# Head 1's keys and queries by seven products in a hybrid decoder trunk; where the replaced block of x is made, and when the out-projection's weight sums run

## The chip, the cores and the metric

The kernel runs on one core of one Trainium2 chip. The metric is the device time of one execution in microseconds (us). A core has five instruction queues that matter here: TensorE (PE, matmuls; PEld is its weight load), VectorE (DVE), ScalarE (ACT), GpSimd (POOL) and SyncE (SP, which only issues DMAs). Each queue runs its instructions in the order in which they stand, and an instruction that waits holds everything behind it in its queue. DMAs are issued from SP, ACT and POOL.

## The reference

One layer: RMS norm, one input projection, three token mixers on disjoint head groups, gates, one output projection with a residual, and a final RMS norm. 512 tokens and 16 learned meta tokens make 528 columns.

```python
h = rms_norm(x, norm_w)
proj = h @ w_in
(dq, dk, dv, dz, db, da, gq, gk, gv, gz, gl, fq, fk, fv, fz, ff) = split_cols(proj)
o_dn  = gated_head_norm(gated_delta_rule_chunked(...), dz, dn_norm_w)   # 6 heads x 128
o_gla = gated_head_norm(gla_chunked(...), gz, gla_norm_w)               # 5 heads, dk 64, dv 128
o_fox = forgetting_attention(fq * 128**-0.5, fk, fv, log_f) * silu(fz)  # 5 heads x 128
x = x + concat([o_dn, o_gla, o_fox]) @ w_out
return rms_norm(x, final_norm_w)[:, N_META:]
```

## The kernel before

**Precision and the unit of work.** Every large product is made from operands split into two parts, hi and lo, and three matmuls: hi by hi, hi by lo, lo by hi. A block is 128 columns of `w_in`; it is loaded in two halves of 512 KB (`load_half`, line 144): SP loads `raw`, ACT casts it into `whi` (line 165), DVE subtracts and gives `wlo` (line 166). `raw`, `whi` and `wlo` have two buffers each. Rows of such halves run through the whole program, and PE eats them in order. x itself stands split in SBUF, as `xh[k]` and `xl[k]` for 16 rows k of 128 channels.

**Order of the program.** First `dz` of four heads and the gates; then DeltaNet in two groups of three heads (`dn_keys`, `dn_values`, `dn_queries`, `dn_inverse`, `dn_mix`); then the five gates `gz` of GLA (line 1304 on); then GLA in three pairs of heads (`gla_pair`); then five heads of forgetting attention (`fox_head`); then the output projection. A scheduler puts the instructions of each queue into their order from the program and a timeline of its own; a few rules pin places: `PLACE` says behind which matmul of which block a matmul of GLA stands, `behind` and `later` do the same by distance, `high_priority` lets splits go first.

**The inverse.** `dn_inverse` inverts 32-row triangles by 60 short DVE operations on the tile `ab` (lines 740 and 742), each of which needs the one before it. The result goes to DRAM and comes back in another layout: `sc<-ab` (744), then `iv<-sc` and `xm<-sc` (747, 749), all issued on ACT's queue, so that ACT stands still between 744 and 747 until the copy has landed. For the second group of heads this runs while PE makes the gates `gz`. In the profile block 25 is `gz` of GLA head 1, 28 that of head 4, 29 the first keys of GLA (`gk`), and `whi29_1` the second half of block 29.

**A gate.** `gate_z` (402): DVE takes the projection out of PSUM (`zgz`, 403), POOL takes a maximum (`stgz`, 385), ACT makes three activations (386 to 388), DVE one product (389).

**Seven products.** `inproj_pair` (558) makes two blocks together from seven half-size products instead of eight, after Winograd's scheme: the columns of x are cut into two halves of 264, its rows k into 0 to 7 and 8 to 15, the weights into four halves. It needs sums of weights in DRAM (`ti`), made early by DMAs on POOL, copies and then adding DMAs (`in_jobs`, `steps_of`, 490 and 492); sums of x (`t`, made by `x_sums` in `gla_pair`); and for its fifth product a replaced block: `x_last` (543) overwrites the upper half of `xh[k]`, `xl[k]`, k below 8, by differences of x. From then on x can't be used whole. `load_half` lets the weight-sum DMAs go in portions: each half allows `rate` cost units of the list `chores`, 1 for a copy and 1.6 for a sum, tied by `paced` behind that half's split in the queue's order.

Before the change the pairs begin with `fv` and `fz` of head 1 (`SKIP` = 1); head 0's four blocks and head 1's keys `fk` and queries `fq` are made whole, with 96 matmuls of 264 columns and 48 of 512. `x_last` stands behind head 1's queries: eight loads `xe` on POOL, then per block two operations on ACT and two on DVE. The output projection uses seven products for eight of its 16 rows, with weight sums `tw`.

## Time and profile before

| | |
|---|---|
| median of three executions | 999.3 us (999.12 to 1000.33) |
| the profiled execution | 997.56 us, span of its core 995.9 us |
| mean granted clock of PE | 0.997 |
| busy PE, DVE, ACT, POOL | 980.4, 666.8, 475.3, 249.0 us |
| gates `gz` of GLA | within 340 to 400 us |
| head 1's keys and queries | 612.08 to 639.4 us |
| pairs by seven products | 639.4 to 815 us |

Times in a row are us from the start of the span; a mean in ns stands in the third view of a group. "Idle before" is the time that the engine did nothing before that row, with an arrow to what ended it. A share of DMA is the mean of the 16 DMA engines. PE's matmuls are pipelined, so rows overlap, and the distance between starts is what one costs.

### The profile page before, as it was taken

The numbers are of one execution on the slowest core, as the hardware profiler recorded it, in microseconds if no ns is written. First come the engines' busy times: TensorE is split into PE (matmuls) and PEld (weight loads), VectorE is DVE, ScalarE is ACT, GpSimd is POOL, SyncE is SP. The second block draws the span as 40 slices with busy tenths as digits, with TensorE's granted clock in tenths as the row PEclk, the third lists the DMA queues.
The fourth block names the chain that finished last, engine by engine and source line by source line (L and its number), as shares of the span: only waits on it lengthen the run. The fifth ranks groups of instructions, "written<-read, shape, count | busy, mean of one in ns | idle before, by whom it ended". The sixth has DMA issues, their size and how long they took to land.

```text
span 995.9 us, 19769 instructions
## 1 busy us (share of the span) xinstructions
PE 980.4 (98%) x7774; PEld 896.6 (90%) x7774; DVE 666.8 (67%) x1443; ACT 475.3 (48%) x1043; POOL 249.0 (25%) x293
## 2 busy tenths in 40 slices
PE   9999999999999999999999999999999999999996
PEld 7899999899999888899999988799999998888885
DVE  6356786966567895434675847776766676877573
ACT  7653533334456234334546444555555554454353
POOL 0031423322233244301313223221221134000060
PEclk9999999999999999999999999999999999999998
DMA  9754666777547688844847866565454577355634
GB/s 346 263 193 168 210 216 238 172 181 173 116 113 169 140 215 198 298 130 144 209 143 190 186 178 178 176 200 161 168 172 135 182 267 273 106 190 199 202 106 169
DMA packets 67489, 186.05 MB, mean 187 GB/s; under 512 B 13725, under 2 KB 16973, under 8 KB 66692
## 3 DMA queue, kind: packets, MB, share of 16 engines
q1 hardware_dynamic: 41920, 121.86, 36.0%
q0 software_dynamic: 16576, 56.83, 23.9%
q10 hardware_dynamic: 8900, 6.10, 2.2%
q8 instruction: 61, 1.00, 0.4%
q14 instruction: 32, 0.26, 0.1%
HBM read 174.07 MB, written 56.69 MB: 232 GB/s over the span
## 4 chain that ended last, share of the span: by engine, by line
PE 70%; DVE 7%; DMA 5%; ACT 3%; issue 2%; POOL 1%; ACTq 0%; DVEq 0%; POOLq 0%
PE pp L240 28%; PE pp_a L571 8%; PE pa L1392 5%; PE pq L1392 4%; PE pt L1392 4%; PE ps L1392 2%; PE pp_b L571 2%; PE pp_d L571 2%; PE pp_c L571 2%; DVE wlo L166 2%; DMA sc<-ab 1%; DMA zd<-gqk 1%; PE pr L1392 1%; PE pss L1041 1%; ACT whi L165 1%
## 5 line engine op out<-in xcount | busy, mean ns | idle before, releaser
L240 PE MATMUL pp<-xh,wlo 128*128 128x264 f32 (+2 forms) x1120 | 272.9, 306 | 2.2 <-DVE wlo L166 2.2
L240 PE MATMUL pp<-xh,whi 128*128 128x264 f32 (+2 forms) x1120 | 273.9, 306 | 0.0
L240 PE MATMUL pp<-xl,whi 128*128 128x264 f32 (+2 forms) x1120 | 272.9, 306 | 0.0
L165 ACT CAST whi<-raw 128x1024 fp32r<-128x1024 f32 x131 | 137.1, 1047 | 157.0 <-PE pp L240 81.2
L166 DVE TENSOR_TENSOR wlo<-raw,whi 128x1024 fp32r<-128x1024 f32 x131 | 160.6, 1226 | 72.8 <-ACT whi L165 64.2
L240 PEld LDWEIGHTS pp<-xh,wlo 128*128 128x128 f32 x1120 | 182.6, 189 | 12.1 <-DVE wlo L166 3.6
L240 PEld LDWEIGHTS pp<-xh,whi 128*128 128x128 f32 x1120 | 182.6, 189 | 9.4 <-ACT whi L165 0.4
L240 PEld LDWEIGHTS pp<-xl,whi 128*128 128x128 f32 x1120 | 182.7, 189 | 8.9 <-issue 0.4
L385 POOL TENSOR_SCALAR stc<-cv 128x528 f32<-128x528 f32 (+1 forms) x18 | 28.9, 1607 | 144.9 <-DVE cv L613 124.4
L613 DVE SCALAR_TENSOR_TENSOR cv<-pb,cpk,cv 128x528 f32<-128x528 f32 (+1 forms) x54 | 41.1, 761 | 0.8
L1417 POOL TENSOR_TENSOR acc<-acc,fw 128x512 f32<-128x512 f32 x4 | 5.8, 1483 | 117.4 <-ACT sqf L1414 117.4
L571 PE MATMUL pp_a<-t,whi 128*128 128x264 f32 (+1 forms) x224 | 30.5, 284 | 0.0
L1392 PE MATMUL pa<-wloo,oh 128*128 128x512 f32 x72 | 28.7, 398 | 0.0
L571 PE MATMUL pp_a<-xh,whi 128*128 128x264 f32 x112 | 28.4, 288 | 0.0
L571 PEld LDWEIGHTS pp_a<-t,whi 128*128 128x128 f32 x224 | 27.9, 189 | 0.5
L1392 PE MATMUL pa<-whio,ol 128*128 128x512 f32 x72 | 28.4, 394 | 0.0
L571 PE MATMUL pp_a<-xl,whi 128*128 128x264 f32 x112 | 28.3, 287 | 0.0
L385 POOL TENSOR_SCALAR stdz<-zdz 128x512 f32<-128x512 f32 x6 | 11.3, 1885 | 62.1 <-DVE zdz L403 62.0
L165 ACT CAST whis<-raws 128x1024 fp32r<-128x1024 f32 x16 | 16.3, 1048 | 21.2 <-PE pq L1392 10.8
L166 DVE TENSOR_TENSOR wlos<-raws,whis 128x1024 fp32r<-128x1024 f32 x16 | 19.2, 1223 | 10.7 <-ACT whis L165 10.6
L1392 PE MATMUL pa<-whio,oh 128*128 128x512 f32 x72 | 26.0, 400 | 0.0
L740 DVE TENSOR_TENSOR ab<-ab 51x30 f32<-51x30 f32 (+14 forms) x60 | 21.2, 354 | 6.4 <-DMA ab<-scr 4.2
(509 smaller groups left out, 2138.6 us busy)
## 6 DMA issues: line engine op xcount, KB each, us to landing
raw<-in_w_in SPq DMA_DIRECT2D x103, 512.0 KB, 3.7
ti<-in_w_in POOLq DMA_DIRECT2D x42, 512.0 KB, 5.5
raw<-ti SPq DMA_DIRECT2D x28, 512.0 KB, 3.3
tw<-in_w_dn POOLq DMA_DIRECT2D x24, 512.0 KB, 5.9
ti<-ti POOLq DMA_DIRECT2D x14, 512.0 KB, 6.3
rawo<-in_w_out SPq DMA_DIRECT2D x13, 512.0 KB, 3.2
raws<-tw SPq DMA_DIRECT2D x12, 512.0 KB, 3.9
xt<-in_xtok SPq DMA_DIRECT2D x8, 512.0 KB, 8.9
```

Source lines behind the costliest of these rows:

```text
L165: pace[0] = A.copy(hi, raw).ins
L166: pace[1] = V.tensor_tensor(out=lo, in0=raw, in1=hi.bitcast(F32), op=ALU.subtract).ins
L240: mm = PE.matmul(p_[:, :nt], wt[:, j * m : (j + 1) * m], xx[k][:, t0 : t0 + nt], start=(k == 0 and wt is hi and xx is xh), stop=(k == KT - ...
L385: maxes.append(G.tensor_scalar_max(t, src, LOW).ins)
L571: m = PE.matmul(p_[:, cols], wt[:, j * P : (j + 1) * P], xx[j][part_][:, cols], start=first and i == 0, stop=i == len(todo) - 1, skip_grou ...
L613: V.scalar_tensor_tensor(out=c, in0=pb[:, t0 + w : w + T], scalar=cwc[:, blk, w : w + 1], in1=c, op0=ALU.mult, op1=ALU.add)
L740: V.tensor_tensor(out=t3, in0=a3[:, j + 1 :, j : j + 1].to_broadcast([NN * 4 + H, m, j]), in1=a3[:, j : j + 1, 0:j].to_broadcast([NN * 4 + ...
L1041: mm = PE.matmul(ps[o0 : o0 + n, b * n : b * n + n], kx[rr, k0 : k0 + n], qx[rr, q0 : q0 + n], start=True, stop=True)
L1392: mm = PE.matmul(p_, o_[:, s], w_, start=(first and n == 0), stop=(last and n == 2), skip_group_check=True)
L1417: G.tensor_tensor(out=acc[tb, cc], in0=acc[tb, cc], in1=fw[cc], op=ALU.mult)
```

## The change

`SKIP` becomes 0, so head 1's `fk` and `fq` become the first pair, with four more halves of `ti`. As this pair comes before x could be replaced, its products have another order: the one on replaced x is the last of seven, and the one for the unused columns gets its own bank `e`. The differences of x are made in `x_early`, two blocks in each of the first three gates `gz` of GLA and one in each of the last two, and go to a DRAM tensor `x3`; `x_last` only fetches them, by 16 DMAs of 132 KB on POOL behind head 0's `fz`. `PLACE` pins the scores of GLA pair 2 within the new pair. The portions allowed to `chores` drop from 1.4 to 0.35 a half from head 1 on, and once the first pair is in the program a sum of weights waits for the split and doesn't only stand behind it.

```diff
-SKIP = 1
+SKIP = 0
...
+        "pss21": (('pair', 0), 22),
+        "pss22": (('pair', 0), 38),
+        "pss23": (('pair', 0), 54),
+        "pss24": (('pair', 0), 72),
+        "pss25": (('pair', 0), 90),
+        "pss26": (('pair', 0), 108),
+        "pg02": (('pair', 0), 128),
...
-        "pss23": (('fk', 1), 60),
-        "pss24": (('fk', 1), 80),
-        "pss25": (('fk', 1), 90),
-        "pgo2": (('pair', 0), 8),
...
-                paced(G.dma_start(out=out_, in_=in_, accum_op=ALU.add, max_dma_last_dim=2048))
+                x = G.dma_start(out=out_, in_=in_, accum_op=ALU.add, max_dma_last_dim=2048)
+                if ("pair", 0) in head:
+                    tc.add_manual_dep(x.ins, pace[1].name, mybir.DependencyInfo(
+                        mybir.DependencyClass.Sync, mybir.DependencyReason.DATA), reason="paced")
+                else:
+                    paced(x)
...
+    x3 = drp.tile([NK, P, T], F32, name="x3")
+
+    def x_early(k):
+
+        r, c = row(f"xe{k}")[:, :T], row(f"xc{k}", F32R)[:, :T]
+        nc.gpsimd.dma_start(out=r.rearrange("p (i t) -> p i t", i=2), in_=xT[:, k : k + 9 : 8, HT:])
+        x12, x22 = r[:, :HT], r[:, HT:]
+        A.activation(x12, x12, AF.Copy, scale=nwc[:, k : k + 1])
+        V.scalar_tensor_tensor(out=x22, in0=x22, scalar=nwc[:, k + 8 : k + 9], in1=x12, op0=ALU.mult,
+                               op1=ALU.subtract)
+        A.copy(c[:, :HT], x22)
+        V.tensor_tensor(out=c[:, HT:], in0=x22, in1=c[:, :HT].bitcast(F32), op=ALU.subtract)
+        nc.gpsimd.dma_start(out=x3[k], in_=c.bitcast(F32))
+
     def x_last():
 
         for k in range(NK):
-            r = row(f"xe{k}")[:, :T]
-            nc.gpsimd.dma_start(out=r.rearrange("p (i t) -> p i t", i=2), in_=xT[:, k : k + 9 : 8, HT:])
...
-            A.copy(xh[k][:, HT:], x22)
-            V.tensor_tensor(out=xl[k][:, HT:], in0=x22, in1=xh[k][:, HT:].bitcast(F32), op=ALU.subtract)
+            for x, o in ((xh, 0), (xl, HT)):
+                nc.gpsimd.dma_start(out=x[k][:, HT:].bitcast(F32), in_=x3[k][:, o : o + HT])
...
-        product(a, w_in[b2, 1], sums("t4"), cols=dead)
-        A.activation(c2[:, dead], a[:, dead], AF.Copy, scale=-1.0)
+        if n > 0:
+            product(a, w_in[b2, 1], sums("t4"), cols=dead)
+            A.activation(c2[:, dead], a[:, dead], AF.Copy, scale=-1.0)
+        else:
+            e = bank("e")
+            product(e, w_in[b2, 1], sums("t4"), True, cols=dead)
+            A.copy(c2[:, dead], e[:, dead])
+            replaced()
+            V.scalar_tensor_tensor(out=c2[:, dead], in0=a[:, dead], scalar=-1.0, in1=c2[:, dead],
+                                   op0=ALU.mult, op1=ALU.subtract)
...
+            done["fz", h] = inproj(("fz", h), meta=False)
+            x_last()
             gate_z("fz", h)
-            evac(inproj(("fk", H1)), ahead_[H1][:, 0])
-            evac(inproj(("fq", H1), meta=False), ahead_[H1][:, 2], scale=float(P) ** -0.5)
-            x_last()
...
-    AHEAD = {(0, -1): (1.4, (-1, -2, -3, -4, -5, -6, -7), (0, 1, 2, 3))}
+    AHEAD = {(0, -1): (1.4, (-1, -2, -3, -4, -5, -6, -7, -8), (0, 1, 2, 3)), ("f", 1): (0.35,)}
...
     for h in range(G1):
         gate_z("gz", h)
+        for i in ((0, 1), (2, 3), (4, 5), (6,), (7,))[h]:
+            x_early(i)
```

The order that the scheduler makes of it, at three places. DVE between the two splits of block 27, while PE makes gate 3 (names: `wlo` the low half of a weight, `ab` the inverse, `zgz1` gate 1, `xe` and `xc` the blocks of x as loaded and as split). Before:

```order
L166 TENSOR_TENSOR wlo27_0_4802<-raw27_0_4799,whi27_0_4801 128x1024
L742 TENSOR_TENSOR ab1_4071<-ab1_4071 51x15x16
L740 TENSOR_TENSOR ab1_4071<-ab1_4071 51x238
L742 TENSOR_TENSOR ab1_4071<-ab1_4071 51x14x17
L740 TENSOR_TENSOR ab1_4071<-ab1_4071 51x234
L742 TENSOR_TENSOR ab1_4071<-ab1_4071 51x13x18
L740 TENSOR_TENSOR ab1_4071<-ab1_4071 51x228
L742 TENSOR_TENSOR ab1_4071<-ab1_4071 51x12x19
L403 TENSOR_TENSOR zgz2_4789<-pp26_0_4726,rstd_102 128x512
L740 TENSOR_TENSOR ab1_4071<-ab1_4071 51x220
L166 TENSOR_TENSOR wlo27_1_4833<-raw27_1_4830,whi27_1_4832 128x1024
```

And now:

```order
L166 TENSOR_TENSOR wlo27_0_4853<-raw27_0_4850,whi27_0_4852 128x1024
L766 TENSOR_TENSOR ab1_4073<-ab1_4073 51x240
L768 TENSOR_TENSOR ab1_4073<-ab1_4073 51x15x16
L392 TENSOR_TENSOR zgz1_4736<-zgz1_4736,stgz1_4738 128x512
L766 TENSOR_TENSOR ab1_4073<-ab1_4073 51x238
L558 SCALAR_TENSOR_TENSOR xe2_4745<-xe2_4745,cpk_94 128x264
L768 TENSOR_TENSOR ab1_4073<-ab1_4073 51x14x17
L766 TENSOR_TENSOR ab1_4073<-ab1_4073 51x234
L561 TENSOR_TENSOR xc2_4746<-xe2_4745,xc2_4746 128x264
L768 TENSOR_TENSOR ab1_4073<-ab1_4073 51x13x18
L766 TENSOR_TENSOR ab1_4073<-ab1_4073 51x228
L166 TENSOR_TENSOR wlo27_1_4884<-raw27_1_4881,whi27_1_4883 128x1024
```

Between the splits stood eight operations of the inverse and the evacuation of gate 2; now there are seven, with gate 1's product and the two operations of block `xe2`.

ACT around the copy of the finished inverse (`whi28_0` to `whi29_1` are casts of successive halves, `stgz3` gate 3, `sc` the copy in DRAM). Before:

```order
L165 CAST whi28_0_4873<-raw28_0_4871 128x1024
L165 CAST whi28_1_4904<-raw28_1_4902 128x1024
L386 ACTIVATE stgz3_4863<-stgz3_4863 128x512
L744 DMA sc21_4143<-ab1_4071 51x1024
L387 ACTIVATE stgz3_4863<-stgz3_4863 128x512
L388 ACTIVATE stgz3_4863<-stgz3_4863 128x512
L165 CAST whi29_0_4951<-raw29_0_4949 128x1024
L747 DMA iv1_4145<-sc21_4143 128x12x32
L749 DMA xm1_4147<-sc21_4143 32x3x32
L165 CAST whi29_1_5006<-raw29_1_5004 128x1024
```

And now:

```order
L165 CAST whi28_1_4962<-raw28_1_4960 128x1024
L557 ACTIVATE xe4_4833<-xe4_4833,cpk_94 128x264
L560 CAST xc4_4834<-xe4_4833 128x264
L770 DMA sc21_4145<-ab1_4073 51x1024
L165 CAST whi29_0_5017<-raw29_0_5015 128x1024
L557 ACTIVATE xe5_4841<-xe5_4841,cpk_94 128x264
L773 DMA iv1_4147<-sc21_4145 128x12x32
L775 DMA xm1_4149<-sc21_4145 32x3x32
L560 CAST xc5_4842<-xe5_4841 128x264
L165 CAST whi29_1_5072<-raw29_1_5070 128x1024
```

The copy `sc` stands behind the same half, `whi28_1`; gate 3's activations, which stood around it, have gone further back, and parts of blocks 4 and 5 of x stand around it in their place, one of them (`xc5`) between the two read-backs and `whi29_1`.

POOL from gate 0's maximum on (`ti` are the input projection's weight sums). Before:

```order
L385 TENSOR_SCALAR stgz0_4648<-zgz0_4646 128x512
L490 DMA ti_680<-ti_680 256x512 x2
L385 TENSOR_SCALAR stgz1_4719<-zgz1_4717 128x512
L490 DMA ti_680<-ti_680 256x512 x2
L385 TENSOR_SCALAR stgz2_4791<-zgz2_4789 128x512
```

And now:

```order
L388 TENSOR_SCALAR stgz0_4650<-zgz0_4648 128x512
L555 DMA xe0_4657<-in_xT 128x2x264
L493 DMA ti_680<-ti_680 256x512
L555 DMA xe1_4665<-in_xT 128x2x264
L562 DMA x3_683<-xc0_4658 128x528
L493 DMA ti_680<-ti_680 256x512
L388 TENSOR_SCALAR stgz1_4738<-zgz1_4736 128x512
L555 DMA xe2_4745<-in_xT 128x2x264
```

The load of `xe2` stands behind gate 1's maximum, which itself now stands behind the store of block 0 to `x3`.

More of the change, by code (lines that the diff above doesn't have):

```diff
@@ L567, in product @@
             third[0] += 1
-            hi, lo = load_half(src, f"{b1}_{len(order)}", raws[0] if third[0] % 3 == 0 and 0 < n and h < FOX_HEADS - 1 else None)
+            hi, lo = load_half(src, f"{b1}_{len(order)}", raws[0] if third[0] % 3 == 0 and 1 < n and h < FOX_HEADS - 1 else None)
             todo = [(hi, j, i) for j in range(NK) for i in range(2)] + [(lo, j, 0) for j in range(NK)]
@@ L1018, in scores @@
             ref = gv[:, :, 0, s - 1 : s].to_broadcast([R, npair, s])
-            V.tensor_tensor(out=dv[:, :, 1, :], in0=gv[:, :, 1, :], in1=ref, op=ALU.subtract)
+            x = V.tensor_tensor(out=dv[:, :, 1, :], in0=gv[:, :, 1, :], in1=ref, op=ALU.subtract)
+            if p == 2 and li == 0:
+                kqs.append(x.ins)
             if s > 1:
```

19 lines of the change are left out of this document (8 added, 11 removed).

## The prediction

> **What bounds the kernel now.** First the page's busy times, then who keeps TensorE (PE) waiting.
>
> ```profile
> PE 980.4 (98%) x7774; PEld 896.6 (90%) x7774; DVE 666.8 (67%) x1443; ACT 475.3 (48%) x1043; POOL 249.0 (25%) x293
> ...
> PE pp L240 <- DVE wlo L166: 2.2, 4, 0.7
> ```
>
> PE is busy for 980.4 of 995.9 us, and its longest named wait, for the low half of a split weight (`wlo`, line 166), adds up to 2.2 us. So a change of the time has to be PE work that goes, or a new place where PE waits. Next, busy time by stage; the columns are PE, PEld, VectorE (DVE), ScalarE (ACT), GpSimd (POOL), clock, DMA share, GB/s.
>
> ```profile
> 340.00:400.00 60.00, 59.49 (x295) 49.65 (x294) 43.85 (x98) 23.75 (x33) 26.09 (x21) 1.00 0.80 190
> 612.00:640.00 28.00, 27.04 (x326) 23.16 (x328) 21.74 (x47) 14.05 (x29) 9.27 (x9) 1.00 0.60 162
> 640.00:815.00 175.00, 174.99 (x1423) 170.64 (x1410) 124.50 (x299) 96.61 (x200) 35.85 (x36) 1.00 0.55 180
> ```
>
> The three rows are the stages that the change touches: GLA's gates, where blocks of x will be made; head 1's keys and queries, where they are made now; and the pairs of blocks by seven products. PE has no idle time to give in the first or the third (59.49 of 60, 174.99 of 175). But the first is not free of limits: DVE is busy there for 43.85 us. Third, the chain of waits, which in this stretch leaves PE.
>
> ```profile
> 384.63 8.81 DMA sc<-ab
> ...
> 394.65 1.06 ACT whi L165
> 395.73 1.24 DVE wlo L166
> 397.01 6.84 PE pp L240 x49
> ```
>
> This is the place that decides my forecast. The DRAM copy of the finished 32-row inverses (`sc<-ab`) is issued by ACT at 384.63; ACT then waits in its own queue for that copy, because the next thing it has to issue reads it back; only then does it make `whi` of block 29's second half (394.65), DVE makes `wlo` (395.73), and PE starts that half at 397.01. PE stands at the end of a chain that begins with DVE's last `ab` operation.
>
> **The matmuls that go and come.** Durations are of this profiled execution.
>
> ```profile
> 111.73 5.82 PE pp L240 x48
> ...
> 702.68 2.94 PE pp_d L571 x24
> ...
> 870.94 11.12 PE pq L1392 x48
> ```
>
> Each row is a run of matmuls without a gap: 48 of 264 columns in 5.82 us, 24 of a product in 2.94, 48 of 512 columns in 11.12. Head 1's keys are 96 of the first kind, 11.64 us, its queries 48 of the last, 11.12: 22.76 us. Seven products are 7 x 2.94 = 20.58. The term is **-2.2 us**. Whether splits keep up with 2.94 us a product (seven now where there were four) is answered by the stage row 640:815: seven such pairs ran there with PE busy for 174.99 of 175. I take nothing for it; bounds 0 and +1 us, the latter being PE's idle time in row 612:640.
>
> **The stall that goes with the blocks of x.** Now they are made between 616 and 654, and once they hold up PE.
>
> ```profile
> 629.42 0.52 ACT L548 ACTIVATE xe<-xe,cpk 128x264 f32<-128x264 f32 x1 [4.93 <-DMA xe<-in_xT]
> 631.43 1.23 DVE L166 TENSOR_TENSOR wlo<-raw,whi 128x1024 fp32r<-128x1024 f32 x1 [4.06 <-ACT whi L165]
> 631.12 0.40 PE L240 MATMUL pp<-xh,wlo 128*128 128x512 f32 x1
> ...
> 632.71 0.50 PE L240 MATMUL pp<-xh,wlo 128*128 128x512 f32 x1 [0.53 <-DVE wlo L166]
> 633.04 0.40 PE L240 MATMUL pp<-xh,whi 128*128 128x512 f32 x1
> 633.66 0.46 PE L1041 MATMUL pss<-kq 64*32 64x32 f32 x32 [0.22 <-DVE kq L1027]
> 634.33 0.46 PE L1041 MATMUL pss<-kq,kq 64*32 64x32 f32 x32 [0.22 <-DVE kq L1027]
> 634.72 0.50 PE L240 MATMUL pp<-xl,whi 128*128 128x512 f32 x1
> ```
>
> ACT sits 4.93 us before an `xe` block whose load has not landed; the `whi` behind it in ACT's queue is late, DVE waits 4.06 us for that, and PE runs dry. From 631.12 to 634.72 PE issues five matmuls of 512 columns (5 x 11.12 / 48 = 1.16 us) and two groups of scores (633.66 to 634.72, less two waits of 0.22: 0.62), and took 3.60 us: 1.8 us are lost. After the change nothing of x is computed there, only fetched, so the term is **-1.8 us** (0 to -1.8; I take the whole, because ACT and DVE lose 8 x (0.52 + 0.41 + 0.48 + 0.42) = 14.6 us of work there and get three more splits, 3 x 2.3 = 6.9). The sixteen fetches into x wait for the last projection that reads x whole (`fz` of head 0), and the product that reads them is now the last of the seven, six products or 17.6 us later. On POOL's queue eight of them stand ahead of the `MEMSET` of GLA pair 2's score tile, which DVE needs here:
>
> ```profile
> 608.86 0.29 DVE L1008 COPY_PREDICATED a<-lmk,psd 128x128 f32<-128x128 uint8 x1
> ```
>
> `fz` is 48 matmuls of 512 columns, 11.1 us, and ends where row 612:640 begins, so its first row of x is used at 601 at the latest and each further one 0.7 us on: the eighth fetch can go at 604 and the memset follows, four before its use. Cost 0; if a fetch had to wait for the weight sums queued ahead on POOL, each microsecond past 608.9 would be one on PE, since DVE's splits queue behind it.
>
> **What GLA's gates have to take.** Eight blocks are now made there, two instructions each on ACT and DVE. The same work today:
>
> ```profile
> L548 ACT ACTIVATE xe<-xe,cpk x8: 501/515/517, 621.8 to 651.4; 128x264 f32<-128x264 f32 x8
> L549 DVE SCALAR_TENSOR_TENSOR xe<-xe,cpk x8: 479/484/1048, 637.9 to 652.7; 128x264 f32<-128x264 f32 x8
> ...
> L554 DVE TENSOR_TENSOR xl<-xe,xh x8: 419/424/434, 639.7 to 653.7; 128x264 fp32r<-128x264 f32 x8
> ...
> DMA to landing us min/median/max: 3.2/5.1/6.8
> ```
>
> A block costs DVE 0.484 + 0.424 = 0.91 us and ACT 0.93, and its load lands 5.1 us after issue (3.2 to 6.8). By the order of instructions five of the eight blocks stand on DVE ahead of the end of the `ab` chain, and one evacuation (0.67) moves behind it. DVE has little room there:
>
> ```profile
> 360.26 2.70 POOL L385 TENSOR_SCALAR stgz<-zgz 128x512 f32<-128x512 f32 x1 [5.76 <-DVE zgz L403]
> ...
> 364.09 0.40 DVE L740 TENSOR_TENSOR ab<-ab 51x240 f32<-51x240 f32 x1
> 365.06 0.69 DVE L389 TENSOR_TENSOR zgz<-zgz,stgz 128x512 f32<-128x512 f32 x1 [0.57 <-ACT stgz L388]
> ...
> 366.42 1.21 DVE L166 TENSOR_TENSOR wlo<-raw,whi 128x1024 fp32r<-128x1024 f32 x1
> ...
> 375.99 0.69 DVE L389 TENSOR_TENSOR zgz<-zgz,stgz 128x512 f32<-128x512 f32 x1 [0.76 <-ACT stgz L388]
> ...
> 383.79 0.18 DVE L742 TENSOR_TENSOR ab<-ab 51x30 f32<-51x30 f32 x1
> 384.62 0.63 ACT L386 ACTIVATE stgz<-stgz 128x512 f32<-128x512 f32 x1 [4.69 <-POOL stgz L385]
> 384.63 0.26 ACTq L744 DMA_DIRECT2D sc<-ab  x1
> ...
> 393.45 0.39 ACTq L747 DMA_DIRECT2D iv<-sc  x1
> ```
>
> Between 344 and 384 it stood still only before the two gate products, 0.57 and 0.76 us, and the chain ended at 383.97. Work alone moves that end by 5 x 0.91 - 0.67 - 1.33 = 2.5 us, if the two old waits are filled. New waits come on top, from the loads: the load of block `xe2` stands on POOL behind gate 1's maximum (2.70 us), which waits for the evacuation. From that evacuation to `xe2` being scaled on ACT are 2.70 + 5.1 + 0.52 = 8.3 us. On DVE there stand between the two only eight `ab` operations (0.40 each, 3.2), one `xc` (0.42), one split (1.21) and the gate's product (0.69): 5.5 us. DVE waits 2.8 us, and the next split, `wlo27_1`, waits behind it. Counted in the same way `xe4` has 7.3 us of work ahead and waits 1.0, `xe0` 7.9 and waits 0.3. Together 2.5 + 4.1 = 6.6 us later. Behind the chain's end ACT issues the copy at once (before it lost 0.66 behind `stgz`), and one more cast (0.41) stands ahead of `whi29_1`: -0.2. With the copy taking 8.8 us again, `wlo29_1` and PE are **+6.4 us** late. PE's shorter wait at `wlo27_1` lies within these 6.4.
>
> Bounds: with loads of 3.2 us the only wait left is 0.9 at `xe2`, and the delay 2.5 + 0.9 - 0.2 = 3.2; if the copy then also takes what the same copy took in the other group of heads,
>
> ```profile
> 209.14 5.70 DMA sc<-ab
> ```
>
> 3.1 us less, 0.1 is left. With loads of 6.8 the waits are 1.9, 4.5 and 2.7, and the delay 11.4. I take 5.1 and 8.8, because the DMA engines there are as full as anywhere:
>
> ```profile
> 355.00:360.00 5.00, 5.00 (x24) 4.05 (x23) 4.79 (x11) 1.70 (x2) 0.00 (x0) 1.00 1.05 178
> ...
> 365.00:370.00 5.00, 5.00 (x23) 4.05 (x23) 4.74 (x10) 1.95 (x2) 0.00 (x0) 1.00 1.06 176
> ...
> 375.00:380.00 5.00, 5.00 (x23) 4.10 (x22) 4.06 (x10) 2.85 (x4) 0.71 (x1) 1.00 1.01 168
> ```
>
> Their share is 1.05, 1.06 and 1.01 in these five-microsecond windows, with one or two sums of weights under way, and those sums continue while 8 loads and 8 stores of 264 KB join them.
>
> The Trainium skill, page "DMA: Bandwidth & Descriptors", section "Anatomy of one DMA — SWDGE (gpsimd) path", prices such a DMA at about 2.0 us plus its bytes over 436 GB/s. For 270 KB that is an estimate of 2.6 us, half of the 5.1 that the trace shows; by it the wait at `xe2` would be 0.3, the delay 2.6, and the whole sum -0.9 us. The trace decides, so I do not use it.
>
> **Other moves.** One more pair puts eight more weight sums and copies on POOL, so the out-projection's sums (`tw`) run later: nine of them now lie beside the pairs.
>
> ```profile
> raw<-ti SPq DMA_DIRECT2D x28, 512.0 KB, 3.3
> ...
> tw<-tw POOLq DMA_DIRECT2D x8, 512.0 KB, 7.4
> ```
>
> A weight of a pair lands in 3.3 us; one that meets a sum may take as long as the sum, 7.4. Two raw buffers let it come about 3 us late, so a meeting costs at most 1 us, nine at most 9, and if none is late, 0. I take 0.5, near the lower end, since one sum in some 18 us meets few loads in their last microsecond. The last sum is issued while head 3's pairs run, before 815, and its readers belong to the products from 870.94 on; a sum's wait for a split also holds POOL's own work, but POOL is idle for four fifths of that stage (35.85 of 175).
>
> **Sum.** -2.2 - 1.8 + 6.4 + 0.5 = +2.9 us on this execution's 997.56 us. That execution was 1.7 below the median of the runs shown, 999.3; on the median, **1002.2 us**. A change under 0.2%, 2 us, cannot be told from none here.
>
> **Rivals.** (1) The inverse's copy lands as fast as at 209, and the loads of x in 3.2 us: the gates cost 0.1, and the sum is -2.2 - 1.8 + 0.1 + 0.5 = -3.4, **995.9 us**. For it: the order was laid out with the blocks spread over the gates, at most two a head, and the splits are still about 5.5 us of DVE work apart. Against it: the DMA shares above, and that the copy took 8.8 in just this place. It is the case on the other side, and it decides from a delay of `wlo29_1` below 1.5 us. (2) Loads land in 3.2 but the copy takes 8.8: delay 3.2, sum -0.3, **999.0 us**, no change to be seen; the skill's price leads here too. (3) The DMA engines, already at 1.0, take 16 transfers more and fall behind: loads of 6.8 us, delay 11.4, sum +7.9, **1007.2 us**. For it the shares; against it, that the raw weights of this stage are wanted only every 5.56 us (half of 11.12) and landed in time so far.
>
> **Chances.** Forecast 0.40, with a range of its own of 1000.5 to 1004.5; (1) 0.27; (2) 0.20; (3) 0.13. Of the forecast 0.06 falls within 0.2%, of (2) 0.14 within and 0.03 on each side, of (1) 0.03 within. So slower 0.34 + 0.13 + 0.03 = 0.50, the same 0.06 + 0.14 + 0.03 = 0.23, faster 0.27. The range, 996 to 1007 us, runs from (1) to (3).
>
> **What would show it.** In the changed profile: products of head 1's pair at 2.94 us without a gap of PE from `fz` on; no `xe` wait on ACT after 600; DVE idle before `xe2` by some 3 us, released by ACT or the load; the second `sc<-ab` issued near 390.7 instead of 384.63; PE's second half of block 29 near 403 instead of 397; in the waits of PE more than 2.2 us on `wlo`. I am wrong if that copy is issued before 388 or PE reaches block 29's second half before 399, or if the pairs' stage has gaps.

## The result, and the profile after

The changed kernel takes **1013.61 us** (median of 4 runs, 1011.55 to 1014.05), the kernel before 999.21 beside it: a ratio of 1.014, with a 95% interval of 1.0122 to 1.0157. It is 14.4 us slower where 2.9 were forecast, and outside the range. The profiled execution took 1013.45 us with a span of 1011.7, against 997.56 and 995.9 before.

First the busy times and PE's waits of the changed kernel (waits: total us, times, longest us).

```profile
PE 983.8 (97%) x7798; PEld 899.9 (89%) x7798; DVE 670.1 (66%) x1449; ACT 481.6 (48%) x1050; POOL 269.6 (27%) x326
...
PE pfx L1264 <- DVE fp L1261: 3.9, 1, 3.9
PE pss L1069 <- issue: 3.5, 3, 1.6
PE pp L243 <- DVE wlo L166: 2.8, 4, 1.2
PE pn L819 <- DVE uf L808: 1.8, 1, 1.8
PE pp L243 <- ACT whi L165: 1.5, 3, 0.9
PE pp_a L585 <- ACT whi L165: 1.4, 1, 1.4
...
PE pp_d L585 <- ACT whi L165: 0.9, 1, 0.9
```

PE is busy for 3.4 us more and the span is 15.9 us longer. Before, the longest wait on a split was 0.7 us; now there are waits of 1.2 and 1.4, one of 1.8 for the inverse (`uf`), and one of 3.9 for `fp`, the softmax of a forgetting head. The waits at GLA's scores `pss`, to which the profile gives no cause, add up to 3.5, against 1.3 before. Line numbers of the changed kernel are up to some 30 higher. Next, the stages (columns as in the prediction: PE, PEld, DVE, ACT, POOL, granted clock, DMA share, GB/s).

```profile
340.00:400.00 60.00, 56.99 (x253) 45.61 (x252) 42.52 (x99) 21.54 (x32) 27.06 (x29) 0.97 0.86 219
622.00:649.00 27.00, 23.96 (x319) 22.51 (x319) 22.98 (x46) 16.07 (x27) 6.95 (x5) 1.00 0.55 162
649.00:824.00 175.00, 170.61 (x1375) 166.46 (x1376) 116.53 (x285) 91.74 (x189) 37.86 (x37) 0.98 0.66 191
```

PE now stands still in all three: 3.0 us in the gates, 3.0 in the new first pair, 4.4 beside the other pairs, which before ran without a gap. And the clock, 1.00 throughout before, is 0.97 and 0.98. Two narrow looks show how; the first and the fourth row are windows with waits, the second and the last follow them.

```profile
381.64:385.05 3.41, 1.59 (x6) 1.02 (x7) 3.34 (x8) 2.21 (x4) 3.24 (x4) 1.00 0.36 65
385.05:388.46 3.41, 3.41 (x10) 2.63 (x9) 3.24 (x9) 1.73 (x3) 1.25 (x2) 0.50 0.89 275
...
422.60:426.02 3.42, 1.83 (x16) 1.62 (x14) 1.10 (x3) 1.66 (x3) 0.62 (x2) 1.00 1.09 258
...
678.59:682.01 3.42, 1.39 (x12) 1.17 (x10) 1.84 (x8) 0.99 (x4) 0.03 (x1) 1.00 0.41 135
682.01:688.83 6.82, 4.95 (x21) 4.74 (x22) 4.56 (x11) 3.34 (x7) 3.27 (x3) 0.50 0.53 167
```

PE stood still for 1.8 of 3.41 us in the first row and 2.0 in the fourth; right behind each the clock is 0.50, for one window and for two. In the third row it stood still for 1.6 us, and the clock stayed. PE was at work for 3.41 + 4.95 = 8.36 us at half clock, so 4.2 us went that way, in work that no row names as a wait. The profile before has no such window between its first microseconds and its last.

The gates themselves went almost as forecast. In the chain of waits:

```profile
391.07 7.28 DMA sc<-ab
...
400.60 1.06 ACT whi L165
401.68 1.24 DVE wlo L166
```

The copy of the inverse went out at 391.07 (forecast 390.7, before 384.63) and `wlo` of block 29's second half was made 5.95 us later than before (forecast 6.4).

### The profile page after: what moved, and what is told of

Read it like the earlier page. It is cut to its first block, busy times and chain, and to the rows that moved or that the text cites. A ratio compares the mean times of both kernels' runs of the same rounds, so it can differ in the third digit from the quotient of the medians.

```text
span 1011.7 us, 19923 instructions
## 1 busy us (share of the span) xinstructions
PE 983.8 (97%) x7798; PEld 899.9 (89%) x7798; DVE 670.1 (66%) x1449; ACT 481.6 (48%) x1050; POOL 269.6 (27%) x326
## 4 chain that ended last, share of the span: by engine, by line
PE 68%; DMA 8%; DVE 6%; issue 3%; ACT 3%; POOL 2%; ACTq 0%; POOLq 0%; SPq 0%; DVEq 0%
PE pp L243 27%; PE pp_a L585 8%; PE pq L1421 4%; PE pa L1421 4%; PE pt L1421 4%; PE ps L1421 2%; PE pp_c L585 2%; PE pp_b L585 2%; PE pp_d L585 2%; DMA xe<-in_xT 2%; DVE wlo L166 1%; DMA sc<-ab 1%; PE pr L1421 1%; DMA raw<-ti 1%; PE pss L1069 1%
## 5 line engine op out<-in xcount | busy, mean ns | idle before, releaser
L243 PE MATMUL pp<-xh,wlo 128*128 128x264 f32 (+2 forms) x1072 | 260.9, 306 | 2.9 <-DVE wlo L166 2.8
L243 PE MATMUL pp<-xh,whi 128*128 128x264 f32 (+2 forms) x1072 | 261.1, 306 | 1.5 <-ACT whi L165 1.5
L243 PE MATMUL pp<-xl,whi 128*128 128x264 f32 (+2 forms) x1072 | 260.6, 306 | 0.0
L166 DVE TENSOR_TENSOR wlo<-raw,whi 128x1024 fp32r<-128x1024 f32 x134 | 164.6, 1228 | 72.2 <-ACT whi L165 60.3
L243 PEld LDWEIGHTS pp<-xh,wlo 128*128 128x128 f32 x1072 | 174.8, 189 | 12.6 <-DVE wlo L166 4.3
L243 PEld LDWEIGHTS pp<-xh,whi 128*128 128x128 f32 x1072 | 174.7, 189 | 10.9 <-ACT whi L165 2.6
L243 PEld LDWEIGHTS pp<-xl,whi 128*128 128x128 f32 x1072 | 175.0, 189 | 8.5 <-issue 0.4
L585 PE MATMUL pp_a<-xh,whi 128*128 128x264 f32 x128 | 32.3, 287 | 1.8 <-ACT whi L165 1.4
L585 PE MATMUL pp_a<-xl,whi 128*128 128x264 f32 x128 | 32.2, 286 | 0.0
L166 DVE TENSOR_TENSOR wlos<-raws,whis 128x1024 fp32r<-128x1024 f32 x16 | 19.2, 1222 | 10.9 <-ACT whis L165 10.8
L585 PEld LDWEIGHTS pp_a<-xh,whi 128*128 128x128 f32 x128 | 24.1, 188 | 2.3 <-ACT whi L165 1.6
```

The costliest lines, as they stand in the source:

```text
L166: pace[1] = V.tensor_tensor(out=lo, in0=raw, in1=hi.bitcast(F32), op=ALU.subtract).ins
L243: mm = PE.matmul(p_[:, :nt], wt[:, j * m : (j + 1) * m], xx[k][:, t0 : t0 + nt], start=(k == 0 and wt is hi and xx is xh), stop=(k == KT - ...
L585: m = PE.matmul(p_[:, cols], wt[:, j * P : (j + 1) * P], xx[j][part_][:, cols], start=first and i == 0, stop=i == len(todo) - 1, skip_grou ...
```

## The experiments

The kernels below were timed beside the kernel before on the same chip. Single profiles of one kernel differ by some microseconds ahead of the place that was edited, so verdicts rest on ratios (0.1% is 1 us; a ratio can differ by 0.1% from that of the two medians), and a profile is used for where and how.

**One part at a time.** First `gates_only`, the kernel before with the blocks of x in the gates and the fetches in `x_last` at its old place:

```diff
+        for i in ((0, 1), (2, 3), (4, 5), (6,), (7,))[h]:
+            x_early(i)
...
+            for x, o in ((xh, 0), (xl, HT)):
+                nc.gpsimd.dma_start(out=x[k][:, HT:].bitcast(F32), in_=x3[k][:, o : o + HT])
```

> The kernel before with one part of the change: the eight differences of x are made in GLA's gates and fetched where they were made before; head 1's keys and queries stay whole, the weight sums keep their pace. The changed kernel ran 6.2 us behind the kernel before at the end of the gates and 9.5 us behind at the end of head 0's fz. Theory A (all of these 9.5 us are the gates' doing, the 3.3 us behind them by way of the inverse that comes late): the gates cost +9.5, the stall at 631 that goes gives 1.8 back: 1007 us. Theory B (the gates cost 6.2, the rest comes from the longer list of weight sums): 1003.6 us.

1002.95 us, ratio 1.0045 (1.0024 to 1.0065), near theory B. The gates are dear, but they explain only about a third of the 1.4%. Then `diff_late`, the changed kernel without them, `x_last` making the differences as before:

```diff
-        for i in ((0, 1), (2, 3), (4, 5), (6,), (7,))[h]:
-            x_early(i)
```

> The changed kernel without its blocks of x in the gates: x_last loads and makes the differences behind head 0's fz as the kernel before did, while the first pair by seven products runs. Theory A: PE reaches fz of head 0 some 9.5 us earlier, and the 14.6 us of ACT and DVE work cost 2 to 4 us in the first pair: 1006 to 1008 us. Theory B: 6.2 us earlier only: 1009.5 to 1011.5 us. If the first pair has no room for that work at all, over 1013 us.

1012.78 us, 1.0142 (1.0107 to 1.0176): no better than the change, and between the expected ranges. In its profile PE starts head 0's `fz` 1.3 us ahead of the kernel before and is 11.6 behind at the end. So something from `fz` on costs 12.9 us there; in the changed kernel's profile, which is 9.5 us behind at `fz`, it is 6.4. And `early_in_gla`, the changed kernel with the same call in `gla_pair(p)`:

```diff
-        for i in ((0, 1), (2, 3), (4, 5), (6,), (7,))[h]:
+        for i in ((0, 1, 2, 3), (4, 5), (6, 7))[p]:
             x_early(i)
```

> The changed kernel with the differences of x made in GLA's three pairs of heads (four blocks, two, two) and not in the gates. DVE is busy there for 26 of 60 us. Theory A: the 9.5 us at the end of GLA go, less up to 2 for the work's new place: 1004 to 1006 us. Theory B: 6.2 go: 1007.5 us. Rival: GLA's own chains of short DVE operations suffer there as the inverse did, and nothing is gained: 1011 us or more.

1018.07 us, 1.02 (1.0169 to 1.0232): the rival's number, and worse than in the gates. In its profile PE waits 4.1 us for a `wlo` and 3.3 for `kq` of GLA between 400 and 600 us; that GLA's short operations hold these up is likely, but was not followed. DVE's share of busy time was no guide.

**The sums beside the pairs.** `no_late_sums`, the changed kernel with this in `steps_of`:

```diff
-            if kind:
+            if kind and ("pair", 0) in head:
+                pass
+            elif kind:
```

> The changed kernel without the out-projection's adding DMAs that come after the first pair has begun (those terms of its weight sums are left out, the output is not the reference's). Theory S (the store of GLA's last gated output, which took 7.5 us beside such a sum where it took 2.7 us before, holds DVE's memset and so the softmax of head 1, and PE stands still and then runs at half clock): without the sums that store takes about 3 us, the stall of 3.9 us and the half clock behind it go, 1006 to 1008 us. Theory O (the store comes late because the order of GLA pair 2 moved into the first pair; the sums are beside the point): 1012 to 1014 us.

1009.66 us, 1.0112 (1.008 to 1.0144): between the two answers, and its interval overlaps that of the change (1.0122 to 1.0157), so the time alone does not decide. But this profile lost 14.7 us up to `fz`, where the instructions are those of the changed kernel (9.5 there), and won 2.7 back behind it, where the changed kernel lost 6.4. The place is this. POOL's and SP's queues of the changed kernel, then DVE's:

```profile
669.19 0.90 POOL L493 DMA_DIRECT2D tw<-tw  x1 [12.14 <-DVE fsm L1250]
...
672.50 1.07 SPq L1162 DMA_DIRECT2D zd<-gqk  x1
...
679.99 0.30 DVE L1250 CUSTOM_DVE_ANT_0 fp<-pfa,fqk 128x144 f32<-128x144 f32 x1 [5.24 <-issue]
680.01 0.06 DVE L1218 MEMSET fqk<- 128x1 f32 x1
...
683.88 0.66 PE L1264 MATMUL pfx<-ident,fp 128*128 128x128 f32 x2 [3.90 <-DVE fp L1261]
```

`zd<-gqk` stores the last gated output of GLA. The memset of head 2's tile `fqk` takes over its buffer, waits for the store, and stands in DVE's queue directly ahead of the next block of head 0's softmax (`fp`; the two starts are 0.02 us apart). Beside the sum `tw<-tw` the store let the memset go 7.5 us after its issue; DVE stood still for 5.2, PE for 3.9, and then PE ran at half clock. Without the sums:

```profile
675.04 0.33 SPq L1164 DMA_DIRECT2D zd<-gqk  x1
...
678.98 0.06 DVE L1220 MEMSET fqk<- 128x1 f32 x1
```

3.9 us, and no wait of `pfx`. It is so in each profile taken: with a sum beside the store 5.7 to 7.5 us from store to memset and a stall of `pfx` of 1.1 to 3.9 (the changed kernel, diff_late, early_in_gla, loads_ahead), without one at most 4.5 us and none (the other eight kernels with the added pair, and 2.75 in the kernel before). `sums_behind` leaves the sums and takes their wait for the split away:

```diff
-                if ("pair", 0) in head:
-                    tc.add_manual_dep(x.ins, pace[1].name, ...Sync...)
-                else:
-                    paced(x)
+                paced(x)
```

> The changed kernel with its thin rate, but the adding DMAs beside the pairs only stand behind the split in the order and do not wait for it. If the wait matters (it lets a sum start just when the loads and stores of the same moment do): 1007 to 1010 us. If it is the sums' own traffic that slows the neighbours: 1012 to 1014 us, no change.

1008.54 us, 1.0098 (1.0066 to 1.013), within the first answer: the wait for a split does about 4 us of harm, though the intervals just overlap. Without it the sums of this profile start at 658.0 and 682.1, one before and one after the store at 672.5. `sums_early`, from the changed kernel, and `late_early`, from `diff_late`, have a higher pace from the start:

```diff
-    AHEAD = {(0, -1): (1.4, ...), ("f", 1): (0.35,)}
+    AHEAD = {(0, -1): (1.6, ...)}
```

> The changed kernel with 1.6 instead of 1.4 units of weight sums a half from the start, and no thin rate behind: by its order the last sum is issued before the first pair by seven products, as in the kernel before; the gates keep the blocks of x. From the run without the late sums: the stretch from the end of head 0's fz to the end of the kernel gave 2.5 us back, where the changed kernel lost 6.4. Theory S (the sums beside the pairs are what is lost there): 1013.6 - 8.9 = 1004.7, plus up to 2 us for the denser sums before: 1004.5 to 1007 us. Theory O (order of the pairs, not the sums): 1012 us or more.

> The same pace of 1.6 with the differences of x made behind head 0's fz and not in the gates. Theory A+S: the gates' 6 us and the sums' 8.9 both go; that work beside the first pair without sums costs 1 to 4 us: 998 to 1002 us. Rival (the 14.6 us of DVE and ACT work do not fit into the first pair, sums or not; the run with late differences lost 13 us from the end of fz on): 1004 us or more.

1011.66 us, 1.0129 (1.0083 to 1.0175), and 1013.3, 1.0138 (1.0094 to 1.0182). The first lies between its two answers, the second has its rival's number, yet not its reason: from `fz` to the end these two profiles differ from the kernel before by -1.8 and +1.0 us, and what they lose, they lose ahead of `fz`. In these profiles a higher pace of the sums moves the loss ahead of the pairs; it does not take it away.

**The added pair without its sums.** `pair_no_sums` is made from the changed kernel, `late_no_sums` from `diff_late`, both with the sums paced as before and the other three products that read sums changed like this one:

```diff
-    AHEAD = {(0, -1): (1.4, (-1, -2, ..., -8), ...), ("f", 1): (0.35,)}
+    AHEAD = {(0, -1): (1.4, (-2, ..., -8), ...)}
-        product(a, ti[n, 1], sums("t2"))
+        product(a, ti[n, 1] if n else w_in[b2, 0][:, :KC], sums("t2"))
```

> The changed kernel without the weight sums of its added pair: the four products that read them read plain weights of the same size, the list of sums is the one of the kernel before with its pace, and nothing waits for a split (the output is not the reference's). The kernel before with the blocks of x in the gates alone stood at 1002.95 us, 4.1 above the kernel before. Theory T (the sums' traffic, eight adding and copying DMAs more and a tail beside the pairs, is what costs the rest of the 14.4): this kernel lies near 1002.95 less 2.2 for the seven products, 1000 to 1003.5 us. Theory P (the pair itself, its order and GLA pair 2's tail inside it): 1007 us or more.

1004.96 us, 1.0052 (1.0029 to 1.0075).

> The same with the differences of x made behind head 0's fz, not in the gates (output not the reference's). Theory T, and room for that work beside the first pair: 997 to 1000 us. Theory R (the 14.6 us of ACT and DVE work find no room beside seven products): 1003 us or more.

1000.05 us, 1.0018 (1.0004 to 1.0032). The first lies between its two answers, nearer to theory T, and the second at theory T's upper end: the added sums, with the thin pace and the wait for a split that go with them, are worth 1.40 - 0.52 = 0.9% with the blocks in the gates and 1.42 - 0.18 = 1.2% with them late. The other way round, `more_sums` is the kernel before with the eight DMAs of one more pair, into a tensor that nothing reads:

```diff
-    AHEAD = {(0, -1): (1.4, (-1, ..., -7), ...)}
+    AHEAD = {(0, -1): (1.6, (-8, -1, ..., -7), ...)}
```

> The kernel before with the eight weight-sum DMAs of one more pair, which nothing reads, and 1.6 instead of 1.4 units a half, so that the list ends at the same place; the result is the reference's. Traffic theory: the eight DMAs alone cost 4 to 9 us: 1003 to 1008 us. Rival (they cost only beside the blocks of x and the first pair by seven products, or by waiting for splits): 998.5 to 1001 us.

1007.63 us, 1.009 (1.007 to 1.011). So the eight DMAs, with the higher pace that fits them in, cost 9 us, with none of the rest. The issue table (512 KB each, median us to landing): before, then with the eight DMAs, then `pair_free` of the next part, which has none of them.

```profile
raw<-in_w_in SPq DMA_DIRECT2D x103, 512.0 KB, 3.7
ti<-in_w_in POOLq DMA_DIRECT2D x42, 512.0 KB, 5.5
```

```profile
raw<-in_w_in SPq DMA_DIRECT2D x103, 512.0 KB, 4.4
ti<-in_w_in POOLq DMA_DIRECT2D x48, 512.0 KB, 6.0
```

```profile
raw<-in_w_in SPq DMA_DIRECT2D x106, 512.0 KB, 4.4
```

The weights read from `w_in` land 0.7 us later in the median, the changed kernel's too (4.4). But `pair_free` has the same 4.4 and takes the time of the kernel before (1.0004), so a later median landing is not how the 9 us arise. In this profile PE does not lose them little by little: of 7.6 us, 5.8 go in one place, some 490 us into the span, where PE waits for DeltaNet's normalised output (`on`) and then runs a window at half clock.

```profile
PE pt L859 <- ACT on L945: 2.9, 1, 2.9
```

All three kernels with 1.6 units a half lose PE time there (waits of 2.1 to 3.8 us in sums_early, late_early and this one), and of the sixteen with 1.4 only early_in_gla does, 0.4 us. So the higher pace is a rival to the number of DMAs, and more_sums does not tell the two apart; eight DMAs more at 1.4 units, with nothing else changed, were not tried.

**The products alone.** `pair_free` is `pair_no_sums` without any differences of x; `pair_quiet` is `pair_free` with the edit of `no_late_sums` too, the last three lines:

```diff
-            x_early(i)
...
-                nc.gpsimd.dma_start(out=x[k][:, HT:], in_=x3[k]...)
+                G.memset(x[k][:, HT:], 0.0)
...
-            if kind:
+            if kind and ("pair", 0) in head:
+                pass
+            elif kind:
```

> The changed kernel without the added pair's weight sums (its products read plain weights, the list and pace of sums are the kernel's before) and without any differences of x (the replaced block is filled with zeros by POOL; the output is not the reference's). What is left is head 1's keys and queries by seven products. By the prediction's terms -2.2 and -1.8 against the kernel before: 995 us. If the blocks of x beside the keys and queries cost what the stage gained without them elsewhere (up to 4.6): 992 to 995 us. Rival (seven products in place of four of other shapes keep PE waiting for splits): 998 us or more.

999.06 us, 1.0004 (0.9992 to 1.0016): the rival's number, seven products for nothing. ACT in that first pair, and PE's longest wait:

```profile
624.61 1.05 ACT L165 CAST whi<-raw 128x1024 fp32r<-128x1024 f32 x1 [0.45 <-DMA raw<-in_w_in]
...
629.82 1.04 ACT L165 CAST whi<-raw 128x1024 fp32r<-128x1024 f32 x1 [3.23 <-DMA raw<-in_w_in]
```

```profile
PE pp_c L580 <- ACT whi L165: 3.0, 1, 3.0
```

The weight of the fifth product, issued at 622.76, landed 7.0 us later, beside two sums issued at 617.00 and 620.47, and PE stood still for 3.0.

> The pair alone (999.06 us) without the three adding DMAs of the out-projection's sums that lie beside the first pair (left out; the output is not the reference's). The order of every instruction is otherwise the same. In the profile of the pair alone a weight of the fifth product landed after 7.0 us beside two such sums, and PE stood still for 3.0 us. Theory M (a product that wants its 512 KB every 2.94 us has no room for a load beside a sum): the stall goes, 995 to 996.5 us, the four microseconds that the prediction had for the products. Rival (the products are worth nothing in any case): 998.5 to 999.5 us.

**994.07 us**, 0.9954 (0.9938 to 0.997). Three sums less, and every other instruction in the same order: 0.5% against pair_free; PE's wait there falls from 3.0 to at most 0.2. From `fz` on the profile of pair_free is 2.4 us shorter than that of the kernel before, and this one 4.7. The kernel before keeps its own sums, so these figures hold three sums fewer as well; what it would take without them was not tried.

```profile
PE pp_e L582 <- ACT whi L165: 0.2, 1, 0.2
```

**What the gates cost.** `loads_ahead`, the changed kernel with each load one gate earlier:

```diff
+        for i in BL[h + 1]:
+            x_load(i)
         for i in BL[h]:
             x_early(i)
```

> The changed kernel with each load of a block of x in the gates issued one gate earlier; nothing else differs. Theory L (the gates cost what DVE and ACT wait for these loads: 0.9, 2.4 and 2.8 us, and the half clock that follows): the copy of the inverse goes out near 387 and not 391, 1008 to 1010 us. Theory W (the work of five blocks itself, and the DMA engines' load): 1012 to 1014 us.

1014.04 us, 1.0151 (1.0116 to 1.0186): theory W's number, nothing won. `gates_no_loads` and `gates_no_work` are `gates_only` with one half of the work each; the first two lines are the one's, the others the other's:

```diff
-        nc.gpsimd.dma_start(out=r..., in_=xT[:, k : k + 9 : 8, HT:])
+        G.memset(r, 0.5)
-        A.activation(x12, x12, AF.Copy, scale=nwc[:, k : k + 1])
-        V.scalar_tensor_tensor(out=x22, ...)
-        A.copy(c[:, :HT], x22)
-        V.tensor_tensor(out=c[:, HT:], ...)
+        G.memset(c, 0.0)
```

> The kernel before with the blocks of x in the gates, each load of a block replaced by POOL filling the tile with a constant, and all else the same (the output is not the reference's); with the loads it stood at 1002.95 us. Theory L (ACT and DVE wait for the loads, with the half clock behind it): 998 to 1000 us. Theory W (the four operations themselves, 0.91 us of DVE and 0.93 of ACT a block, and the stores): 1001.5 to 1003 us.

> The kernel before with the blocks of x in the gates, loads and stores kept, but without the two operations on ACT and the two on DVE of each block (POOL fills the tile that is stored; the output is not the reference's). With all of it 1002.95 us, without the loads alone 1003.6. Theory W (the operations between the inverse's chain and the splits cost it): 996 to 999.5 us. Theory D (the stores, or either half of the traffic, cost it): 1001.5 to 1003.5 us.

1003.6 us, 1.0039 (1.0019 to 1.0059), and 1002.74, 1.002 (0.9995 to 1.0046; its runs spread from 993.9 to 1007.1). Neither half of the work, taken away, gives the time back for certain. The profiles show part of why (that of gates_no_work is of its slowest execution): first and last operation of the inverse's chain, then the copy and the two read-backs, of gates_only, of gates_no_loads and of gates_no_work.

```profile
343.49 0.20 DVE L746 TENSOR_TENSOR ab<-ab 51x30 f32<-51x30 f32 x1 [2.49 <-DMA ab<-scr]
...
388.86 0.18 DVE L748 TENSOR_TENSOR ab<-ab 51x30 f32<-51x30 f32 x1
```

```profile
341.13 0.20 DVE L746 TENSOR_TENSOR ab<-ab 51x30 f32<-51x30 f32 x1 [2.14 <-DMA ab<-scr]
...
385.10 0.18 DVE L748 TENSOR_TENSOR ab<-ab 51x30 f32<-51x30 f32 x1
```

```profile
343.69 0.20 DVE L741 TENSOR_TENSOR ab<-ab 51x30 f32<-51x30 f32 x1 [3.75 <-DMA ab<-scr]
...
383.68 0.18 DVE L743 TENSOR_TENSOR ab<-ab 51x30 f32<-51x30 f32 x1
...
384.53 0.26 ACTq L745 DMA_DIRECT2D sc<-ab  x1
...
395.34 0.39 ACTq L748 DMA_DIRECT2D iv<-sc  x1
395.76 4.79 ACTq L750 DMA_DIRECT2D xm<-sc  x1
```

The chain takes 45.6 us with everything, 44.1 without the loads and 40.2 without the operations, as long as before (40.15). DVE within the chain, before, in gates_only and in gates_no_loads (busy time and instructions, then clock, DMA share and GB/s as above):

```profile
343.82:383.97 40.15, 37.34 (x84) 1.00 0.88 203
```

```profile
343.49:389.04 45.55, 39.42 (x93) 0.96 0.91 224
```

```profile
341.13:385.28 44.15, 42.93 (x99) 1.00 0.90 225
```

Of the 5.4 us that gates_only adds, 2.1 are work (39.42 against 37.34) and 3.3 are idle time (6.1 against 2.8); the longest waits in it are two for blocks of x (1.07 and 3.77). Without the loads the idle time is 1.2, but the order then has the operations of seven blocks within the chain and not of five, and DVE is busy for 3.5 us more than in gates_only: the work took the place of the waits. Without the operations the loads started earlier, the copy took 10.8 us (8.8 before), and ACT needed 4.8 us to issue the second read-back; `whi` behind them was as late as ever (400.64; 400.93 in gates_only). What exactly holds the issue for 4.8 us is open, and so is what the faster executions of gates_no_work did. `dn_early` is `gates_only` with the blocks in DeltaNet's second group, behind its keys and behind its values; `readback` is `gates_only` with the read-backs of the inverse, this one and `xm`, on POOL:

```diff
+            for i in (0, 1, 2, 3):
+                x_early(i)
         dn_values(g, st)
...
+            for i in (4, 5, 6, 7):
+                x_early(i)
         dn_queries(g, st)
...
-        nc.scalar.dma_start(out=xc, in_=sc2[...])
+        nc.gpsimd.dma_start(out=xc, in_=sc2[...])
```

> The kernel before, with the differences of x made in DeltaNet's second group (four blocks behind the keys, four behind the values) and fetched where they were made; all sums as before, the result is the reference's. There DVE is busy for 37 of 60 us and the DMA engines for 0.55, and no chain of short operations ends in a copy that ACT waits for until 100 us later. Theory A (what the gates cost is their own: the inverse's chain, the copy in ACT's queue, full DMA engines): nothing is lost there and the 2 to 4.6 us that the stage of head 1's keys gained without that work stay: 994.5 to 997 us, faster than both kernels. Theory W (such a block costs PE about 0.8 us wherever it is made, by loads that ACT waits for): 1000 to 1003 us.

1006.66 us, 1.0075 (1.0045 to 1.0104): theory A falls. The blocks of x cost time at each of the three earlier places that were tried; here PE waited for `kd` and `pb` of DeltaNet (1.1 and 1.5 us), still, 1.9 us, behind the copy, and 3.0 in the out-projection.

> The kernel before with the blocks of x in the gates (1002.95 us), and the two read-backs of the finished inverse issued by POOL and not by ACT, so that ACT casts weights while the copy lands. Theory C (the late copy in ACT's queue is how the gates' delay reaches PE): PE no longer waits for whi of block 29's second half (1.0 and 0.5 us, with a window of half clock, 1.7 us, behind it): 999.5 to 1001 us. Rival (PE then waits for the inverse itself at its pinned place, 2 us): 1002 to 1004 us.

1017.0 us, 1.0175 (1.0139 to 1.021), worse than either answer. PE waited 4.4 us for `whi` and 4.7 at the inverse; POOL had loads and sums ahead of the read-backs. So POOL's queue is a worse place for them; whether ACT's queue is how the late copy reaches PE stays open.

**One pair fewer.** `skip2`, the kernel before with head 1's values and gate whole too and the sums of six pairs:

```diff
-SKIP = 1
+SKIP = 2
+                evac(inproj(("fv", h)), v)
+                evac(inproj(("fz", h), meta=False), zr)
+                x_last()
```

> The step the other way: the kernel before with one pair fewer, head 1's values and gate made whole too, six pairs' weight sums at 1.25 units a half, differences of x made behind them; the result is the reference's. PE gets 2.2 us of matmuls more. Theory of traffic, if it goes on below the kernel before as above it (8.7 us a pair): 991 to 995 us, faster than both kernels. Rival (the DMA engines have just enough room in the kernel before, the cost begins with the added pair): 1000 to 1003 us.

1014.0 us, 1.0135 (1.01 to 1.0171), and it does not tell the theories apart. Up to the end of head 1's queries PE ran 3 us ahead of the kernel before; then it waited four times for `xh` (0.95, 1.1, 1.9 and 1.6 us), where the blocks of x are now made, and again in the out-projection (5.6 us). What one pair fewer is worth with its blocks well placed was not tried. No kernel that computes the reference beat the kernel before.

## Why the prediction was wrong

The ratios give the change as a sum: the products alone +0.04%, the blocks of x in the gates +0.48% (pair_no_sums against pair_free; +0.45% on the kernel before), the added sums and their pacing +0.88% (the change against pair_no_sums; +0.90% on the kernel before).

| term | forecast | measured |
|---|---|---|
| products and the stall of x | -2.2 - 1.8 | +0.4 us beside the out-projection's sums, -4.6 with three of these left out |
| blocks of x in the gates | +6.4 | +4.5 to +4.8 |
| weight sums and their pacing | +0.5 | +8.8 |

**The direction and the gates** were right, by the mechanism that was named. The chain lasted 46.7 us (40.15 before, 343.82 to 383.97), 6.6 more, the very 6.6 of the forecast. That the sum is met so well is luck, for its parts were not: DVE was busy in the chain for 39.49 us, 2.2 more than before, where the forecast had 3.9 (4.55 of work less 0.67), and idle for 4.4 more, where it had 2.8 (4.1 of new waits less 1.33 of old ones). `xe0` and `xe2` waited 0.9 and 2.4 us (0.3 and 2.8 forecast), `xe4` not at all (1.0), and `xe3`, which the forecast had not priced, 2.8: its load took 11.4 us, well past the bound of 6.8. From the chain of waits, the chain's two ends and that load; then DVE's three waits:

```profile
344.29 0.20 DVE ab L766
...
368.35 11.41 DMA xe<-in_xT
...
390.85 0.19 DVE ab L768
```

```profile
358.94 0.49 DVE L558 SCALAR_TENSOR_TENSOR xe<-xe,cpk 128x264 f32<-128x264 f32 x1 [0.87 <-ACT xe L557]
...
372.58 0.49 DVE L558 SCALAR_TENSOR_TENSOR xe<-xe,cpk 128x264 f32<-128x264 f32 x1 [2.35 <-ACT xe L557]
...
380.33 0.49 DVE L558 SCALAR_TENSOR_TENSOR xe<-xe,cpk 128x264 f32<-128x264 f32 x1 [2.77 <-ACT xe L557]
```

PE then lost its time earlier than said, at the splits of blocks 27 and 28, and did not wait at block 29 any more; its first matmul on that `wlo` started 5.95 us late (402.96 instead of 397.01).

**The step that failed is "Other moves"**: "so a meeting costs at most 1 us, nine at most 9, and if none is late, 0. I take 0.5". The term measured 8.8 us. Two things are wrong in it. It priced only the nine sums that now lie beside the pairs, not what eight DMAs more and their pace cost elsewhere: more_sums has no sum beside a pair at all and loses 9 us. And the price of a meeting was taken from one load's slack; measured, one meeting cost 3.0 us (pair_free) and another 3.9 plus half clock, the second through a store that the prediction never looked at. How the 8.8 us divide between the number of DMAs, their pace and their wait for a split is open; sums_behind puts the last at about 4.

**"Whether splits keep up with 2.94 us a product ... I take nothing for it"** is the second. The row 640:815 showed pairs without a gap, but with no sum under way; the two last ones landed at 618.5 and 625.1, under the whole blocks of head 1's keys, where a half lasts 5.82 us and a product 2.94. With sums there the four microseconds were gone; with three of them left out the kernel was 4.6 us faster than the kernel before (994.07). That fits the terms -2.2 and -1.8 and a condition that was missed, but the 4.6 also hold what the three sums cost by themselves, so the size of the two terms is not shown. Rival (3), DMA engines that fall behind, named a related cause, in another stage and at half the size.

**Waits were priced at their length.** Where PE stood still for 1.8 and 2.0 of 3.41 us, it ran the next window or two of 3.41 us at half clock, and each such window of work takes 1.7 us longer. In the changed profile that is 4.2 us, none in the forecast. The Trainium skill, page "TensorE: Matmul & The Clock Gate", section "Part 1: The HAM clock gate (the "warmup" mystery)", states a free-running window of 3413 ns and that the clock falls after one idle window. The trace agrees with the window (3.41 and 6.83 us at 0.50) and not with the rule: 1.8 us of idle time were enough.

Two statements of "What would show it" did not hold: the first pair has four gaps, and the pairs' stage has gaps, which the prediction had named as a sign of being wrong.

## What to carry to other kernels

Price a prepared operand by all its DMAs, not by the matmuls that it saves: here eight DMAs of 512 KB and the pace that fits them in cost 9 us, and the products that they feed saved nothing until three other sums were left out. A stage that ran without gaps proves that its loads keep up only with the traffic that ran beside it, so look at what will be under way then, stores and buffers' next owners among it. And count idle time of PE by windows: here waits that fill more than about half of 3.4 us cost 1.7 or more behind them.

## What the runs showed of the hardware

The clock. Over the 17 profiles that have such drops ahead of their last microseconds, PE's idle time was added up in windows of 3.413 us at full clock, on the grid that the drops themselves give. All 28 windows with 1.85 us or more of it were followed by half clock; of 23 with 1.38 to 1.85 us, 10 were; of some 4,800 with less, one was (1.11 us, 237.85 to 241.26 of late_early). Drops lasted one to three windows.

An issue of a DMA is not always short: 4.8 us on ACT for the second read-back of gates_no_work, 1.45 in the changed kernel, 0.7 in the kernel before.

A median landing time is not a price. The weights from `w_in` landed in 3.7 us in the kernel before and in 4.4 in both more_sums, at 1.009 of its time, and pair_free, at 1.0004. What counted was which load or store a queue had to wait for.
